# Turning the first token tile in front of the mixer by transfers and VectorE instead of TensorE

## The chip, the cores and the metric

The kernel runs on one core of a Trainium2 chip. A core has TensorE (PE in the profile; PEld is its weight load), VectorE (DVE), ScalarE (ACT), GpSimd (POOL), and queues that issue transfers (SP's above all). The engines run beside each other; each takes its own instructions strictly in the order in which they were written, and waits on semaphores for the others. PE writes to PSUM, from where ACT and DVE fetch. The metric is the device time of one execution in microseconds, the median over runs.

## The reference

Two layers over 256 tokens with 1024 features, all in float32. What surrounds the change, in each layer:

```python
h = layer_norm(ALPHA * h + 0.5 * swiglu(h, ffn1_gate[l], ffn1_up[l], ffn1_down[l]), ln_g[l, 0], ln_b[l, 0])
z = h @ w_in[l]
cb, cc, ch, rq, rf, ri, rg, pu = jnp.split(z, split_at, axis=-1)
...
f = lb + (1.0 - lb) * jax.nn.sigmoid(f_logit.astype(f32))
k = 1.0 - f
...
h = layer_norm(ALPHA * h + mix, ln_g[l, 1], ln_b[l, 1])
h = layer_norm(ALPHA * h + cross_attn(h, mem, ...), ln_g[l, 2], ln_b[l, 2])
h = layer_norm(ALPHA * h + 0.5 * swiglu(h, ffn2_gate[l], ...), ln_g[l, 3], ln_b[l, 3])
```

The mixer is what lies between z and mix: a short gated convolution, a gated recurrence with forget gate f and input k = 1 - f, and a pooling over windows.

## The kernel before

**Number format.** Each float32 operand of a product is split into a rounded high part and a low part that is the rest (`split`, L74 to L77: ACT casts, DVE subtracts). A product is the sum of high by high, high by low and low by high. Weights come from memory into one of six buffers `raw` of 128x1024 (`load`, L79), are split into `whi` and `wlo`, and the buffer is free once the DVE subtraction has read it. So the order on DVE also sets when the next load may be issued.

**Layout.** Tokens lie in two tiles of 128 (h[0], h[1], tokens on the partitions). For products over the features a tile must be turned, so that features lie on the partitions: xT, with high part xTh and low part xTl, 8 blocks of 128 features by 256 tokens. `transposed_half` (L196) turns four blocks of 128x128 on PE into a bank of PSUM and splits them from there; `transposed` (L204) does both halves. The second tile is turned with its tokens reversed (unit `jdn`). Banks of PSUM with the tag `acc` are four.

**Around the change.** `ffn` computes the first feed-forward block, whose last part is `finish` (L328). `finish` ends the down projection tile by tile: `tile_done(0)` adds, normalizes and writes h[0]; then `tile_done(1)` the same for h[1]. Amid the products for tile 1 stands `turn_first` (L343), which turns tile 0 on PE: 8 transposes. In layer 0 this goes through `transposed`; in layer 1 (`prompt`), through `later_split` (L335), where the rounding is done at once and the low parts (`low_part`, L349) are put into gaps of the normalization. `finish` returns a function that turns tile 1 later.

Then `keys` (L933) computes half of the attention's keys from the memory tokens, four groups of 16 or more products into `acc` banks, each fetched by `add` (L150): ACT copies one half to `sums`, DVE adds the other. Before the fourth group tile 1 is turned. Then `mixer` (L957) begins: `columns(1280, 512, ...)` loads w_in for f, splits it in four parts that are held behind the normalization (two of them behind the first turned half of tile 1), and multiplies with xT. PE's first product that needs xT stands there. `ev_f` (L985) then makes f (sigmoid on ACT, a multiply-add on DVE) and k = 1 - f on DVE (L993). `columns(768, ...)` and further loads of w_in follow in the same way.

The order on each engine is what a scheduler made of the program when it was built; `issue_after` only holds instructions behind a given one. Inside the mixer's recurrence PE's order is written by hand (L1054).

Elsewhere the kernel turns tiles by transfers already: four transfers deal the columns of a tile to the four groups of 32 partitions, and one DVE instruction transposes all blocks of 32x32 (`turn`, L520 to L531, for the feed-forward activations; L1231 and L1292 in the mixer).

Of the kernel before, what the change touches and what calls it, by code (L numbers as in the profile page):

```python
# [8 lines left out]
F32 = mybir.dt.float32  # L9
# [8 lines left out]
P = 128  # L18
# [42 lines left out]
def model(ctx: ExitStack, tc: tile.TileContext, t: dict, out: bass.AP):  # L61
# [133 lines left out]

    def transposed_half(src, i, j, dh, dl, unit=idn, keep=None):  # L196
        pt = acc((P, 4, P))
        for k in range(4):
            turns.append(nc.tensor.transpose(pt[:, k, :], src[:, (4 * j + k) * P : (4 * j + k + 1) * P], unit))  # L199
# [4 lines left out]
    def transposed(src, i, dh, dl, unit=idn, keep=None):  # L204
        for j in range(2):
            transposed_half(src, i, j, dh, dl, unit, keep)
            if not j:
                halfway.append(lows[-1])
# [118 lines left out]

    def finish(mm, y, scale, gb, units, last=False, junk=None, ahead=None, prompt=False):  # L328

# [19 lines left out]
        def low_part(w):  # L349
            lows.append(nc.vector.tensor_tensor(w[1], w[2], w[0].bitcast(F32), op=ALU.subtract))  # L350
# [3 lines left out]
        def tile_done(i):  # L354
# [10 lines left out]
            for c in pieces:  # L365
# [45 lines left out]
            for c in pieces:  # L411
# [3 lines left out]
                if last:  # L415
                    e = nc.scalar if c.start == 512 else nc.sync
                    e.dma_start(out[0, tok(i), c], h[i][:, c])

        if ahead is None:
            tile_done(0)  # L420
            tile_done(1)
        else:
            split(*ahead.todo[0])
            if prompt:
                nc.scalar.copy(ahead.todo[1][0], ahead.todo[1][2])
                held.append(ahead.todo[1])
            with tc.issue_after(lows[-1].ins):
                tile_done(0)
            with tc.issue_after(normed[-1].ins):
                if prompt:  # L430
                    split(*ahead.todo[2])
                    split(*ahead.todo[3])
                tile_done(1)
                if not prompt:
                    for x in ahead.todo[1:]:
                        split(*x)
            if prompt:
                with tc.issue_after(normed[-1].ins):
                    low_part(held.pop())
        return lambda keep=None: transposed(h[1], 1, xTh, xTl, units[1], keep)  # L440

# [34 lines left out]
    def ffn(l, name, n, pend=None, last=False, early=None, started=None, following=None):  # L476
        gate, up, down = (t[f"{name}_{x}"][l] for x in ("gate", "up", "down"))
        with tc.tile_pool(name="ffn", bufs=2, reuse_waits="tile") as fp:
# [445 lines left out]

            ahead = following() if following else None
            return ahead, finish(tail, ys, 0.5, gb, (idn, jdn) if name == "ffn1" else (pdn, pdn), last, None if last else squares, ahead, ahead is not None and name == "ffn1")


# [28 lines left out]
    def mixer(l, fill):  # L957
        w_in = t["w_in"][l]
        with tc.tile_pool(name="mix", bufs=1, reuse_waits="tile") as mp:

            def columns(c0, ncol, take, behind=lambda p: None, after=()):
                with ExitStack() as queued:
                    for x in after:
                        queued.enter_context(tc.issue_after(x.ins))
                    w = load(w_in, 0, NK, c0, ncol, hold=bool(after))
                    for n, x in enumerate(w.todo):
# [18 lines left out]
            def ev_f(p):  # L985
                c = slice(2 * p, 2 * p + 2)
                nc.scalar.activation(f[:, :, c, :], f[:, :, c, :], AF.Sigmoid)
                for hh in (2 * p, 2 * p + 1):
# [3 lines left out]
                    )  # L992
                nc.vector.tensor_scalar(  # L993
                    k[:, :, 2 * p : 2 * p + 2, :], f[:, :, 2 * p : 2 * p + 2, :], -1.0, 1.0,
                    op0=ALU.mult, op1=ALU.add,
                )
# [7 lines left out]
            def values_by_halves():  # L1004
                w = load(w_in, 0, NK, 1792, 512)
                for i in range(NT):
# [183 lines left out]
            products_of_others(1)  # L1190
            w_gate = load(w_in, 0, NK, 2304, 512)

# [106 lines left out]

            return project_back([slab(a) for a in (0, 6, 2, 4)], 3, gb, 1.0, idn)  # L1300

# [159 lines left out]
```

## Time and profile before

| | |
|---|---|
| median of 3 runs | 1064.27 us (1064.23 to 1064.66) |
| profiled execution: span from first to last instruction | 1061.1 us |
| TensorE busy in the span | 1051.2 us |
| ScalarE busy in the span | 662.0 us |
| bytes moved by transfers | 251.06 MB, mean 237 GB/s |
| layer 0: end of the first feed-forward block to the mixer | about 165 to 200 us |
| layer 1: the same | about 688 to 724 us |

The profiled execution has no time of its own beside its span; the timed runs lie 3.2 us above it. In the rows of the order of time the first number is the start in the span, the second the duration, then engine, line, operation, what is written<-what is read, and a count where equal instructions follow each other; in brackets stands the idle time before it and who ended it. In the rows of groups, the numbers behind the bar are the busy time of the group in us and the mean of one in ns.

### The profile page before, as it was taken

To read this page: it belongs to the slowest core of one execution; us is meant where nothing else is said; L and a number is where in the kernel's file an instruction comes from. 1 tells how busy PE (TensorE), PEld (TensorE's weight loads), DVE (VectorE), ACT (ScalarE), POOL (GpSimd) and SP (SyncE) were. 2 spreads that over 40 slices of the span, in tenths; PEclk is the share of its full clock that TensorE was granted. 3 is DMA by queue.
4 is the path that set the end of the run, shared out by engine and by line. 5 is a ranking of instruction groups with operands and counts; after the bars stand their busy time and mean duration, and the time that the engine had idled before them with its cause. 6 is when DMAs were issued, how large, how long until landed. Compare 5 with 4: busy or idle time off the path is not lost.

```text
span 1061.1 us, 16496 instructions
## 1 busy us (share of the span) xinstructions
PE 1051.2 (99%) x6014; PEld 934.8 (88%) x6014; DVE 933.2 (88%) x1246; ACT 662.0 (62%) x909; POOL 94.7 (9%) x128
## 2 busy tenths in 40 slices
PE   9999999999999999999999999999999999999996
PEld 7888888889899888889888888998998998888896
DVE  6998898989988789887898987999899787898787
ACT  6675775676557566655665656666774655675661
POOL 8002001000000001010001001010000000000001
PEclk9999999999999999999999999999999999999999
DMA  9999984854675589988789978866636675799971
GB/s 364 296 320 280 260 272 146 268 166 155 210 271 179 171 281 231 363 192 217 239 305 254 338 224 208 271 233 222 206 122 215 241 243 162 242 303 294 241 194 68
DMA packets 142306, 251.06 MB, mean 237 GB/s; under 512 B 11249, under 2 KB 51985, under 8 KB 142225
## 3 DMA queue, kind: packets, MB, share of 16 engines
q1 hardware_dynamic: 130656, 228.89, 65.0%
q0 software_dynamic: 10992, 19.94, 10.9%
q10 hardware_dynamic: 576, 1.18, 0.3%
q8 instruction: 47, 0.77, 0.3%
q14 instruction: 35, 0.28, 0.1%
HBM read 234.50 MB, written 1.05 MB: 222 GB/s over the span
## 4 chain that ended last, share of the span: by engine, by line
PE 92%; DVE 3%; DMA 2%; issue 2%; ACT 1%; POOL 0%; DVEq 0%; ACTq 0%; POOLq 0%
PE acc L132 61%; PE dn L132 27%; DVE wlo L76 2%; PE acc L199 1%; DMA raw<-in_ffn_gate_dram 1%; DMA raw<-in_ffn_down_dram 1%; ACT whi L75 0%; PE dn L1139 0%; DVE raw L702 0%; PE dn L1213 0%; DMA lng<-in_ln_g_dram 0%; DMA h<-in_x_dram 0%; DVE al L76 0%; PE acc L581 0%; DVE square L531 0%
## 5 line engine op out<-in xcount | busy, mean ns | idle before, releaser
L75 ACT CAST whi<-raw 128x1024 fp32r<-128x1024 f32 (+1 forms) x452 | 456.1, 1042 | 201.2 <-PE dn L132 58.0
L76 DVE TENSOR_TENSOR wlo<-raw,whi 128x1024 fp32r<-128x1024 f32 (+1 forms) x452 | 534.5, 1211 | 53.1 <-ACT whi L75 47.1
L132 PE MATMUL acc<-whi,xT 128*128 128x512 f32 (+1 forms) x1064 | 313.9, 372 | 0.0
L132 PEld LDWEIGHTS acc<-whi,xT 128*128 128x128 f32 x1064 | 199.0, 189 | 26.9 <-DVE xT L76 0.3
L132 PE MATMUL acc<-wlo,xT 128*128 128x512 f32 (+1 forms) x532 | 197.9, 372 | 0.0
L132 PE MATMUL dn<-whi,ah 128*128 128x512 f32 x346 | 131.5, 380 | 0.0
L132 PE MATMUL dn<-wlo,ah 128*128 128x512 f32 x346 | 131.3, 379 | 0.0
L132 PE MATMUL dn<-whi,al 128*128 128x512 f32 x346 | 131.1, 379 | 0.0
L132 PE MATMUL acc<-xT,whi 128*128 128x512 f32 x480 | 117.6, 381 | 0.0
L132 PEld LDWEIGHTS acc<-wlo,xT 128*128 128x128 f32 x532 | 100.6, 189 | 13.4
L132 PEld LDWEIGHTS acc<-xT,whi 128*128 128x128 f32 x480 | 86.8, 190 | 9.8
L132 PE MATMUL dn<-whi,xT 128*128 128x512 f32 x288 | 87.7, 380 | 0.0
L132 PEld LDWEIGHTS dn<-wlo,ah 128*128 128x128 f32 x346 | 65.4, 189 | 9.6 <-DVE wlo L76 0.6
L132 PEld LDWEIGHTS dn<-whi,al 128*128 128x128 f32 x346 | 65.4, 189 | 9.2
L132 PEld LDWEIGHTS dn<-whi,ah 128*128 128x128 f32 x346 | 65.4, 189 | 9.0
L132 PEld LDWEIGHTS acc<-xT,wlo 128*128 128x128 f32 x480 | 62.9, 191 | 3.2
L132 PE MATMUL acc<-xT,wlo 128*128 128x256 f32 x480 | 63.2, 275 | 0.0
L132 PE MATMUL acc<-wlo,kTh 128*128 128x512 f32 (+1 forms) x176 | 61.7, 351 | 0.0
L132 PE MATMUL acc<-whi,kTl 128*128 128x512 f32 (+1 forms) x176 | 61.7, 351 | 0.0
L132 PE MATMUL acc<-whi,kTh 128*128 128x512 f32 (+1 forms) x176 | 61.7, 351 | 0.0
L132 PEld LDWEIGHTS dn<-whi,xT 128*128 128x128 f32 x288 | 54.4, 189 | 7.6
L132 PE MATMUL dn<-wlo,xT 128*128 128x512 f32 x144 | 54.6, 379 | 0.0
(252 smaller groups left out, 1296.8 us busy)
## 6 DMA issues: line engine op xcount, KB each, us to landing
raw<-in_ffn_up_dram SPq DMA_DIRECT2D x88, 512.0 KB, 5.7
raw<-in_ffn_down_dram SPq DMA_DIRECT2D x88, 512.0 KB, 5.6
raw<-in_ffn_gate_dram SPq DMA_DIRECT2D x84, 512.0 KB, 5.6
raw<-in_w_in_dram SPq DMA_DIRECT2D x48, 512.0 KB, 4.8
dealt<-sg SPq DMA_DIRECT2D x80, 128.0 KB, 4.5
raw<-in_ffn_up_dram POOLq DMA_DIRECT2D x19, 512.0 KB, 6.3
raw<-in_ffn_gate_dram POOLq DMA_DIRECT2D x16, 512.0 KB, 9.4
raw<-in_ca_k_dram SPq DMA_DIRECT2D x16, 512.0 KB, 5.2
```

What stands on the lines that cost most here:

```text
L75: rounded = nc.scalar.copy(hi, src)
L76: lows.append(nc.vector.tensor_tensor(lo, src, hi.bitcast(F32), op=ALU.subtract))
L132: turns.append(nc.tensor.matmul(o, w, x, start=start, stop=stop, skip_group_check=more))
L199: turns.append(nc.tensor.transpose(pt[:, k, :], src[:, (4 * j + k) * P : (4 * j + k + 1) * P], unit))
```

## The change

In front of the mixer, in both layers:

- Tile 0 is no longer turned on PE. When h[0] is normalized, ACT copies it in two halves of 512 columns into a spare tile, with the features regrouped (every eighth column lies beside the next); four transfers on SP deal it to the four groups of 32 partitions in a second spare tile; after tile 1 is normalized, one DVE instruction transposes the blocks of 32x32 into a third; ACT rounds this into xTh and DVE takes the low part, both reading it with the tokens regrouped (a step of 32 floats).
- So block k of xT now holds the features k, k + 8, k + 16 and so on. Tile 1 is still turned on PE, but reads every eighth column of h[1]; w_in is loaded in the same order of features (`across`, eight rows of the matrix next to each other in a partition).
- In layer 1 the low part of the fourth key weight tile takes the place in the gap of the normalization that a low part of xT had.
- k = 1 - f is made by ACT, not DVE.

```diff
-    def transposed_half(src, i, j, dh, dl, unit=idn, keep=None):
+    def transposed_half(src, i, j, dh, dl, unit=idn, keep=None, grouped=False):
         pt = acc((P, 4, P))
-        for k in range(4):
-            turns.append(nc.tensor.transpose(pt[:, k, :], src[:, (4 * j + k) * P : (4 * j + k + 1) * P], unit))
+        for k in range(4 * j, 4 * j + 4):
+            of_k = src[:, k::NK] if grouped else src[:, k * P : (k + 1) * P]
+            turns.append(nc.tensor.transpose(pt[:, k - 4 * j, :], of_k, unit))
...
-                        None if last or not i or not n else turn_first,
+                        None if last or squares_of or not i or not n else turn_first,
...
+        def turn_by_squares():
+            x, y, o = squares_of()
+            for n in range(2):
+                c = slice(n * 512, n * 512 + 512)
+                nc.scalar.copy(
+                    y[:, c].rearrange("p (g k j) -> p g k j", g=2, j=32),
+                    h[0][:, c].rearrange("p (g j k) -> p g k j", g=2, j=32),
+                )
+            x = x.rearrange("p (b c) -> p b c", b=4)
+            for g in range(4):
+                nc.sync.dma_start(x[g * 32 : g * 32 + 32], y[:, g * 256 : (g + 1) * 256])
+            o = o.rearrange("p (k t) -> p k t", t=P)
+
+            def rest():
+                nc.vector.transpose(
+                    o.rearrange("p k (b r) -> p b k r", b=4), x.rearrange("p b (k j) -> p b k j", j=32)
+                )
+                split(
+                    *(y[:, :, tok(0)].rearrange("p k (r b) -> p k r b", b=4) for y in (xTh, xTl)),
+                    o.rearrange("p k (b r) -> p k r b", b=4),
+                )
+
+            return rest
+
         if ahead is None:
             tile_done(0)
+            rest = turn_by_squares() if squares_of else None
             tile_done(1)
+            if rest:
+                with tc.issue_after(normed[-1].ins):
+                    rest()
...
+                if squares_of:
+                    rest = turn_by_squares()
                 if prompt:
                     split(*ahead.todo[2])
-                    split(*ahead.todo[3])
+                    if squares_of:
+                        nc.scalar.copy(ahead.todo[3][0], ahead.todo[3][2])
+                        held.append(ahead.todo[3])
+                    else:
+                        split(*ahead.todo[3])
...
                 with tc.issue_after(normed[-1].ins):
-                    low_part(held.pop())
+                    if squares_of:
+                        rest()
+                    else:
+                        low_part(held.pop())
...
-                    w = load(w_in, 0, NK, c0, ncol, hold=bool(after))
+                    w = load(w_in, 0, NK, c0, ncol, hold=bool(after), across=True)
...
-                nc.vector.tensor_scalar(
-                    k[:, :, 2 * p : 2 * p + 2, :], f[:, :, 2 * p : 2 * p + 2, :], -1.0, 1.0,
-                    op0=ALU.mult, op1=ALU.add,
+                nc.scalar.activation(
+                    k[:, :, 2 * p : 2 * p + 2, :], f[:, :, 2 * p : 2 * p + 2, :], AF.Copy, scale=-1.0, bias=1.0
                 )
```

The other loads of w_in (for the values and the gate) get `across=True` too, and `squares_of` hands out three spare tiles of the feed-forward block's pool, named squares.

How it moves the instructions on the engines: first ACT in layer 0, from the squares of tile 0's normalization (the activation into kTh) on; h_72 is tile 0, h_73 tile 1. Before:

```order
L392 ACTIVATE kTh,mv<-h_72,mv 128x1024
L75 CAST whi<-raw 128x1024 x2
L75 CAST xT<-acc 128x4x128 x2
L75 CAST whi<-raw 128x1024 x3
L392 ACTIVATE kTh,mv<-h_73,mv 128x1024
L75 CAST whi<-raw 128x1024
L152 COPY sums<-acc 128x256 x2
L75 CAST kTh<-sums 128x512
L75 CAST xT<-acc 128x4x128
```

and the same place now:

```order
L393 ACTIVATE kTh,mv<-h_72,mv 128x1024
L424 COPY squares<-h_72 128x512
L75 CAST whi<-raw 128x1024
L424 COPY squares<-h_72 128x512
L75 CAST whi<-raw 128x1024 x4
L393 ACTIVATE kTh,mv<-h_73,mv 128x1024
L152 COPY sums<-acc 128x256
L75 CAST whi<-raw 128x1024
L152 COPY sums<-acc 128x256
L75 CAST xT<-squares 128x8x128
L75 CAST kTh<-sums 128x512
L75 CAST xT<-acc 128x4x128 x2
```

The two casts of tile 0 from PSUM are gone; two copies stand ahead of tile 1's squares, and one cast of the whole tile ahead of kTh and of tile 1's casts.

DVE in layer 0, from the last step of tile 1's normalization to the second key group's low part. Before:

```order
L412 SCALAR_TENSOR_TENSOR h_73<-h_73,rs,lnb 128x512 x2
L153 TENSOR_TENSOR sums<-acc,sums 128x256
L76 TENSOR_TENSOR wlo<-raw,whi 128x1024
L153 TENSOR_TENSOR sums<-acc,sums 128x256
L76 TENSOR_TENSOR wlo<-raw,whi 128x1024
L76 TENSOR_TENSOR kTl<-sums,kTh 128x512
L76 TENSOR_TENSOR xT<-acc,xT 128x4x128
L153 TENSOR_TENSOR sums<-acc,sums 128x256
L76 TENSOR_TENSOR xT<-acc,xT 128x4x128
L76 TENSOR_TENSOR wlo<-raw,whi 128x1024 x2
```

and now:

```order
L413 SCALAR_TENSOR_TENSOR h_73<-h_73,rs,lnb 128x512 x2
L434 STREAM_TRANSPOSE squares<-squares 128x4x8x32
L153 TENSOR_TENSOR sums<-acc,sums 128x256 x2
L76 TENSOR_TENSOR wlo<-raw,whi 128x1024
L76 TENSOR_TENSOR xT<-squares,xT 128x8x128
L76 TENSOR_TENSOR kTl<-sums,kTh 128x512
L76 TENSOR_TENSOR xT<-acc,xT 128x4x128 x2
L153 TENSOR_TENSOR sums<-acc,sums 128x256 x2
L76 TENSOR_TENSOR wlo<-raw,whi 128x1024 x2
L76 TENSOR_TENSOR kTl<-sums,kTh 128x512
L76 TENSOR_TENSOR wlo<-raw,whi 128x1024 x3
```

The transposing and the low part of tile 0 stand ahead of tile 1's low parts, and three of the four wlo of the mixer's first load have moved behind these.

DVE in layer 1, from the same step to tile 1's low parts. Before:

```order
L412 SCALAR_TENSOR_TENSOR h_73<-h_73,rs,lnb 128x512 x2
L350 TENSOR_TENSOR xT<-acc,xT 128x4x128
L153 TENSOR_TENSOR sums<-acc,sums 128x256
L76 TENSOR_TENSOR wlo<-raw,whi 128x1024
L153 TENSOR_TENSOR sums<-acc,sums 128x256
L76 TENSOR_TENSOR wlo<-raw,whi 128x1024
L76 TENSOR_TENSOR kTl<-sums,kTh 128x512
L76 TENSOR_TENSOR xT<-acc,xT 128x4x128 x2
```

and now:

```order
L413 SCALAR_TENSOR_TENSOR h_73<-h_73,rs,lnb 128x512 x2
L434 STREAM_TRANSPOSE squares<-squares 128x4x8x32
L153 TENSOR_TENSOR sums<-acc,sums 128x256
L76 TENSOR_TENSOR wlo<-raw,whi 128x1024
L76 TENSOR_TENSOR xT<-squares,xT 128x8x128
L153 TENSOR_TENSOR sums<-acc,sums 128x256
L76 TENSOR_TENSOR wlo<-raw,whi 128x1024
L76 TENSOR_TENSOR kTl<-sums,kTh 128x512
L76 TENSOR_TENSOR xT<-acc,xT 128x4x128 x2
```

The second add into sums, which frees a bank of PSUM, now stands behind the low part of the whole tile.

More of the change, by code (lines that the diff above doesn't have):

```diff
@@ L925, in ffn @@
             ahead = following() if following else None
-            return ahead, finish(tail, ys, 0.5, gb, (idn, jdn) if name == "ffn1" else (pdn, pdn), last, None if last else squares, ahead, ahead is not None and name == "ffn1")
+            return ahead, finish(tail, ys, 0.5, gb, (idn, jdn) if name == "ffn1" else (pdn, pdn), last, None if last else squares, ahead, ahead is not None and name == "ffn1", (lambda: [fp.tile([P, DM], F32, tag=f"spare{n}", name="squares", bufs=1) for n in range(3)]) if name == "ffn1" else None)
     def key_weights(l, c, hold=False):
```

16 lines of the change are left out of this document (9 added, 7 removed).

## The prediction

> **What bounds the kernel now.** I read first the head of the page, then who waits for whom on TensorE, then the instructions in order of time on each engine where the mixer begins.
>
> ```profile
> span 1061.1 us, 16496 instructions
> ...
> PE 1051.2 (99%) x6014; PEld 934.8 (88%) x6014; DVE 933.2 (88%) x1246; ACT 662.0 (62%) x909; POOL 94.7 (9%) x128
> ...
> PE dn L562 <- DVE kTh L557: 1.5, 1, 1.5
> PE acc L581 <- DMA h<-in_x_dram: 0.4, 1, 0.4
> ```
>
> The reader is to see that TensorE (PE) is busy 99% and waits for others only at the very start, 1.9 us in all. So work taken off PE shortens the run by what it took there, and any new wait of PE lengthens it one for one. VectorE (DVE), at 88%, has little room where its work is moved. The span is 1061.1 us and the median of the timed runs 1064.27; the 3.2 us between lie outside the span, and I add my sum to the median.
>
> **What is removed: eight transposes in each layer.** PE in order of time, layer 0, then the same place in layer 1:
>
> ```profile
> 170.96 1.04 PE L199 MATMUL acc<-idn,h 128*128 128x128 f32 x8
> 171.75 0.46 PE L132 MATMUL dn<-whi,ah 128*128 128x512 f32 x1
> 172.05 0.38 PE L132 MATMUL dn<-wlo,ah 128*128 128x512 f32 x1
> ...
> 185.78 1.67 PE L132 MATMUL acc<-xT,whi 128*128 128x512 f32 x7
> ...
> 693.94 1.04 PE L338 MATMUL acc<-idn,h 128*128 128x128 f32 x8
> ...
> 695.03 0.38 PE L132 MATMUL dn<-wlo,ah 128*128 128x512 f32 x1
> ...
> 705.27 1.04 PE L199 MATMUL acc<-jdn,h 128*128 128x128 f32 x8
> 706.06 1.76 PE L132 MATMUL acc<-mT,whi 128*128 128x512 f32 x7
> ```
>
> Products of 512 columns start (1.67 - 0.38)/6 = 0.22 us apart (seven of them at 185.78, one at 172.05). From 170.96 to 172.05 PE did the transposes and one product: 172.05 - 170.96 - 0.22 = **0.87 us** a layer, 1.75 in both (layer 1: 695.03 - 693.94 - 0.22 = 0.87). That is all the change can gain. The first product that needs xT starts at 185.78; without the transposes PE would be there at 184.91.
>
> **What is added: instructions that read with a step.** ScalarE (ACT) copies h with a step of 8 floats (2 x 512 columns); DVE transposes 128x1024 read contiguously; ACT rounds it and DVE takes the low part, both reading with a step of 32 floats. The rows next to these:
>
> ```profile
> L76 DVE TENSOR_TENSOR wlo<-raw,whi 128x1024 fp32r<-128x1024 f32 x36 | 43.1, 1218 | 1.6 <-ACT whi L75 1.2 <-DMA raw<-in_ca_k_dram 0.2
> L75 ACT CAST whi<-raw 128x1024 fp32r<-128x1024 f32 x38 | 38.6, 1052 | 5.1 <-PE dn L132 3.8 <-DMA raw<-in_w_in_dram 1.2
> L229 DVE STREAM_TRANSPOSE turned<-early 128x512 f32<-128x512 f32 x2 | 2.1, 1091 | 0.0
> L75 ACT CAST ah<-sg 128x256 fp32r<-128x256 f32 x2 | 1.6, 872 | 0.0
> L76 DVE TENSOR_TENSOR al<-sg,ah 128x256 fp32r<-128x256 f32 x2 | 1.6, 838 | 0.0
> L531 DVE STREAM_TRANSPOSE square<-dealt 128x512 f32<-128x512 f32 x2 | 1.3, 687 | 0.0
> L75 ACT CAST kTh<-sums 128x512 fp32r<-128x512 f32 x2 | 1.2, 617 | 1.9 <-DVE sums L153 1.9
> ```
>
> Contiguous, ACT takes 617 ns for 512 columns and 1052 for 1024: 0.85 ns a column and 0.18 us fixed; DVE by its 687 and 1218 takes 1.04 ns a column and 0.15 us. The split of ah reads s with a step of 4 floats (L804 to L808) and takes 872 and 838 ns for 256 columns: (872 - 180)/256 = (838 - 150)/256 = **2.7 ns a column** on both engines. L229 reads with a step of 8 floats: (1091 - 150)/512 = 1.84 ns. So:
> - copy of 512: from 0.62 (contiguous) to 1.56 us (2.7 ns). I take 1.14, by L229, which has the same step.
> - rounding of 128x1024: from 1.05 to 2.94; low part: from 1.22 to 2.90 us. I take 2.94 and 2.90, by the split of ah, which is the same pair of instructions with such a read.
> - transposing 128x1024: 0.15 + 1.04 x 1.024 = 1.22 us, as L531 reads and writes in the same way.
>
> **Layer 0: when xT is whole.** ACT, then DVE, in order of time before the change; starts in a queue lie 0.06 to 0.1 us closer than the durations say.
>
> ```profile
> 170.51 1.99 ACT L75 CAST whi<-raw 128x1024 fp32r<-128x1024 f32 x2 [2.31 <-PE dn L132]
> 172.41 1.07 ACT L75 CAST xT<-acc 128x512 fp32r<-128x512 f32 x2
> 173.37 2.96 ACT L75 CAST whi<-raw 128x1024 fp32r<-128x1024 f32 x3
> 176.21 1.16 ACT L392 ACTIVATE kTh<-h,mv 128x1024 fp32r<-128x1024 f32 x1
> ...
> 178.89 1.41 DVE L412 SCALAR_TENSOR_TENSOR h<-h,rs,lnb 128x512 f32<-128x512 f32 x2
> 180.22 0.41 DVE L153 TENSOR_TENSOR sums<-acc,sums 128x256 f32<-128x256 f32 x1
> 180.55 1.21 DVE L76 TENSOR_TENSOR wlo<-raw,whi 128x1024 fp32r<-128x1024 f32 x1
> ...
> 184.75 0.69 DVE L76 TENSOR_TENSOR xT<-acc,xT 128x512 fp32r<-128x512 f32 x1
> 185.36 2.35 DVE L76 TENSOR_TENSOR wlo<-raw,whi 128x1024 fp32r<-128x1024 f32 x2
> ```
>
> 1. ACT's queue now has copy, whi, copy, whi x4 ahead of the squares of tile 1: from 170.40, 1.06 + 0.95 + 1.06 + 3.80, so the squares start at 177.27, not 176.21. Tile 1's normalization on DVE hangs on them and ends 1.06 later; the transposing starts at 180.22 + 1.06 = 181.28 and ends at 182.4.
> 2. ACT rounds from 182.5 to 185.45; behind it queue kTh and both casts of tile 1. Meanwhile DVE does two sums and one wlo (2.0 us, hidden), then waits. Low part 185.5 to 188.3, kTl 0.60, the low part of tile 1's first half 0.60: 189.6.
> 3. PE's first product with xT starts at **189.6, not 185.78: +3.8**. The gain of 0.87 is in that, since PE only waits longer.
> 4. Before, the low parts of the four weight tiles were done by 187.7. Now one is done when PE starts; the next ends at 191.9 (0.6 + 0.67 + 1.13 later). PE's new order takes other products between them; followed row by row, waits of 0.2, 0.05 and 0.2 are left: +0.5. Layer 0: **+4.3 us**.
>
> **Layer 1.**
>
> ```profile
> 702.64 0.69 DVE L350 TENSOR_TENSOR xT<-acc,xT 128x512 fp32r<-128x512 f32 x1
> ...
> 704.71 0.42 DVE L153 TENSOR_TENSOR sums<-acc,sums 128x256 f32<-128x256 f32 x1
> ...
> raw<-in_w_in_dram SPq DMA_DIRECT2D x48, 512.0 KB, 4.8
> dealt<-sg SPq DMA_DIRECT2D x80, 128.0 KB, 4.5
> ```
>
> Here the normalization comes 0.87 earlier (702.64 - 0.87 = 701.8). Copies end at 694.5 and 696.5, SP issues the four transfers until 697.2, and by dealt<-sg (same size) the last lands 4.5 later, at 701.7: just in time. Transposing to 703.0, rounding 703.07 to 706.0, low part to 708.9. Behind it on DVE stands the second sums, which ends at 709.3, not 705.1. That add frees a bank of PSUM that PE's fourth group of key products needs: PE waits until **709.3, not 706.06: +3.2**, and nothing is late afterwards. Both layers: 4.3 + 3.2 = **+7.5 us**.
>
> **Edits that I cost at nothing.** k = 1 - f goes from DVE to ACT:
>
> ```profile
> 196.29 0.41 DVE L993 TENSOR_SCALAR k<-f 128x512 f32<-128x512 f32 x1
> ...
> 163.89 0.37 SPq L103 DMA_DIRECT2D raw<-in_w_in_dram  x1
> 172.85 1.50 SPq L103 DMA_DIRECT2D raw<-in_w_in_dram  x2
> ...
> L987 ACT ACTIVATE f<-f 128x512 f32<-128x512 f32 x2 | 1.3, 630 | 1.5 <-DVE f L153 1.4
> ```
>
> DVE gains 0.33 us twice a layer and ACT pays 0.63; PE waits for neither there. Without that cover it is worth -0.7 to +1.3 us a layer. On SP the transfers stand behind the four w_in loads of f, the last issued at 163.89. The copies end at 171.5 and 173.5, so SP is through with the four at 174.9, and the next load, issued at 172.85 before, waits for that; PE doesn't wait for its landing. Loads of w_in by contiguous rows of a partition move the same bytes in as many issues; their landing of 4.8 us could move by some tenths, which reaches PE through the weights of layer 0: between -0.5 and +1 us. POOL's memset of AT comes later and is needed 40 us later.
>
> The eight transposes of tile 1 now load their weights with a step of 8 floats. The rows show only contiguous ones:
>
> ```profile
> L199 PEld LDWEIGHTS acc<-jdn,h x16: 138/140/142, 182.1 to 705.9; 128*128 128x128 f32 x16
> ```
>
> They start 0.1 us apart (0.79 us for eight). By the 2.7 ns a column above, a load would take 0.35, and eight 2.0 us more a layer; by the moving side nothing, as products that pick columns 256 floats apart run at the 0.22 us spacing. In the forecast both ends cost 0: PE has 3 to 4 us of waiting right behind them. If that cover is gone they cost up to 1.7 us. The Trainium skill, "Advanced Engine Details and Errata", section "SBUF Cachelines", says that reads which go to a different 16-byte line each time are penalized, whichever engine reads; by that rule the loads pay the 2.0 us, without it 0. No row here shows it for weights.
>
> **The rivals.**
> 1. *Not slower: the steps cost nothing here.* Copies 0.62, rounding 1.05, low part 1.22. Layer 0: ACT isn't later, the transposing ends at 181.4, and two sums, wlo, low part, kTl and tile 1's first low part (4.1 us) end at 185.5, 0.3 before 185.78; the wlo of step 4 are then late by 1.2 to 1.4: +1.0. Layer 1: the second sums ends at 705.9: -0.2. Together +0.8: 1065.0. Between this and the next rival it decides at about 1.25 ns a column, where the sum passes 2.1 us. Against it: 872 and 838 ns for 256 columns.
> 2. *The milder step*, 1.84 ns everywhere: rounding and low part 2.06 each, +2.7 and +1.5: 1068.5.
> 3. *DVE hides it all.* If xT and the banks were ready when PE comes (184.9 and 705.2; my chains end 4.7 and 4.1 us later), only the transposes would be left: 1064.27 - 1.75 = 1062.5. The chain is one queue on DVE with nothing to drop, which speaks against it.
> 4. *PE's clock falls back* in the waits. At the start PE takes twice as long:
>
> ```profile
> 4.41 1.09 PE L581 MATMUL acc<-pdn,h 128*128 128x128 f32 x4 [0.38 <-DMA h<-in_x_dram]
> 6.68 1.04 PE L581 MATMUL acc<-pdn,h 128*128 128x128 f32 x8
> core 0: 1061.1 us, clock 0.998
> ```
>
> Four transposes took what eight take later, and a mean of 0.998 is 2.1 us lost. A second such stretch in each layer costs up to 2.1 each: 1064.27 + 7.5 + 4.2 = 1076.0. The Trainium skill, "TensorE: Matmul & The Clock Gate", section "HAM oscillation — how this bites in real kernels", puts the point at an idle gap of about 3.4 us; by that rule my waits of 3.8 and 3.2 us straddle it.
>
> **How the numbers follow.** Forecast +7.5 (2.7 ns): 0.45, 1071.8. Milder step: 0.25. Clock or a transfer that lands later than 4.5: 0.10. No cost of steps: 0.15. All hidden: 0.05. A difference under 0.2% (2.1 us) can't be told from no change. Slower: 0.45 + 0.25 + 0.10 = 0.80; within: 0.17, from the last two; faster 0.03, if the gain is larger than the rows show. The range leaves out the last case and the far end of the clock: 1065.0 to 1075.5.
>
> **What would show it.** The casts and low parts of xT from the transposed tile at 2.9 us, copies at 1.1; PE waiting some 3.8 us for the low part of xT in layer 0 and some 3.2 us for sums in layer 1, and nowhere else. Casts near 1.1 us would prove the steps wrong; a PE wait on wlo or on a transfer, the order of my steps.

## The result, and the profile after

| | before | with the change |
|---|---|---|
| median of 6 runs each | 1063.91 us (1062.95 to 1064.66) | 1067.1 us (1066.95 to 1068.52) |
| ratio | | 1.0033 (1.0022 to 1.0045) |
| span of the profiled execution | 1061.1 us | 1066.8 us |

The change makes the kernel 3.2 us slower by the medians; the ratio gives 3.5 us, between 2.3 and 4.8. The forecast was 7.5 us. The head of the page after, and all of TensorE's waits (engine, what it wanted to write, line; who it waited for; us in total, times, longest):

```profile
span 1066.8 us, 16483 instructions
...
PE 1052.6 (99%) x5998; PEld 934.3 (88%) x5998; DVE 936.6 (88%) x1242; ACT 670.6 (63%) x915; POOL 95.0 (9%) x128
```

```profile
PE acc L132 <- DVE sums L153: 1.9, 1, 1.9
PE acc L132 <- DVE xT L76: 1.7, 1, 1.7
PE dn L600 <- DVE kTh L595: 1.5, 1, 1.5
PE acc L619 <- DMA h<-in_x_dram: 1.0, 2, 0.6
PE acc L200 <- DVE sums L153: 0.6, 1, 0.6
```

Before, the list held only kTh (1.5) and h (0.4). Three waits are new, 4.2 us in all. In layer 0 the second half of tile 1's turning (L200) waits for a bank that an add of `sums` frees, and the first product with xT waits for xT's low part; in layer 1 the fourth group of key products waits for a bank. Here they stand in order of time; ACT, DVE and PE of layer 0:

```profile
170.86 1.15 ACT L424 COPY squares<-h 128x512 f32<-128x512 f32 x1 [2.21 <-DVE h L413]
...
177.69 1.16 ACT L393 ACTIVATE kTh<-h,mv 128x1024 fp32r<-128x1024 f32 x1
...
182.96 2.12 ACT L75 CAST xT<-squares 128x1024 fp32r<-128x1024 f32 x1 [2.55 <-DVE squares L434]
...
181.69 1.24 DVE L434 STREAM_TRANSPOSE squares<-squares 128x1024 f32<-128x1024 f32 x1
182.85 0.72 DVE L153 TENSOR_TENSOR sums<-acc,sums 128x256 f32<-128x256 f32 x2
...
185.11 2.01 DVE L76 TENSOR_TENSOR xT<-squares,xT 128x1024 fp32r<-128x1024 f32 x1 [0.41 <-ACT xT L75]
187.04 0.67 DVE L76 TENSOR_TENSOR kTl<-sums,kTh 128x512 fp32r<-128x512 f32 x1
187.63 1.28 DVE L76 TENSOR_TENSOR xT<-acc,xT 128x512 fp32r<-128x512 f32 x2
...
183.29 0.71 PE L200 MATMUL acc<-jdn,h 128*128 128x128 f32 x4 [0.65 <-DVE sums L153]
...
188.37 1.78 PE L132 MATMUL acc<-xT,whi 128*128 128x512 f32 x7 [1.75 <-DVE xT L76]
```

And of layer 1:

```profile
708.48 1.95 DVE L76 TENSOR_TENSOR xT<-squares,xT 128x1024 fp32r<-128x1024 f32 x1 [0.79 <-ACT xT L75]
710.35 0.41 DVE L153 TENSOR_TENSOR sums<-acc,sums 128x256 f32<-128x256 f32 x1
...
707.90 1.04 PE L200 MATMUL acc<-jdn,h 128*128 128x128 f32 x8
710.82 2.34 PE L132 MATMUL acc<-mT,whi 128*128 128x512 f32 x7 [1.87 <-DVE sums L153]
```

The chain is the one that the prediction walked: copies, squares of tile 1, transposing, rounding, low part, and behind it kTl and tile 1's low part in layer 0, the second add of `sums` in layer 1. But rounding takes 2.12 and 2.16 us and the low part 2.01 and 1.95, not 2.94 and 2.90. The copies take 1.15 us each, as forecast. The four transfers land 2.8 to 3.2 us after their issue and are never waited for.

Not all of the loss stands in the list of waits: 4.2 less the 1.75 us of transposes would be 2.5. In layer 0 the low parts of w_in are late too (step 4 of the prediction). The first line is the kernel before, the second the change, the third a group of the page after (weight loads of the products of xT with these low parts), which waits 0.9 us for `wlo`; before, no such wait stood there:

```profile
193.42 1.89 PE L132 MATMUL acc<-xT,whi 128*128 128x512 f32 x8
```

```profile
196.59 1.89 PE L132 MATMUL acc<-xT,whi 128*128 128x512 f32 x8
```

```profile
L132 PEld LDWEIGHTS acc<-xT,wlo 128*128 128x128 f32 x480 | 63.4, 191 | 4.2 <-DVE wlo L76 0.9
```

Ahead of these lines TensorE did the same 47 products with xT: from 185.78 to 193.42 before, 7.64 us, and from 188.37 to 196.59 now, 8.22 us. These 0.58 us and the three waits, less the transposes, make 3.0 to 3.1 us.

The two spans differ by more than the medians do. The changed kernel's profiled execution is its slowest of six. Its time is 1.7 us above its span, and by the same 1.7 us the profiled execution before took 1062.8 us, below all six of its runs. So differences between traces are up to 2.5 us larger here than those between medians; where it matters, below, I compare medians.

### The profile page after: what moved, and what is told of

Its sections match the earlier page's. It is cut to its first block, busy times and chain, and to the rows that moved or that the text cites. A ratio compares the mean times of both kernels' runs of the same rounds, so it can differ in the third digit from the quotient of the medians.

```text
span 1066.8 us, 16483 instructions
## 1 busy us (share of the span) xinstructions
PE 1052.6 (99%) x5998; PEld 934.3 (88%) x5998; DVE 936.6 (88%) x1242; ACT 670.6 (63%) x915; POOL 95.0 (9%) x128
## 3 DMA queue, kind: packets, MB, share of 16 engines
HBM read 234.50 MB, written 1.05 MB: 221 GB/s over the span
## 4 chain that ended last, share of the span: by engine, by line
PE 95%; ACT 2%; DVE 2%; issue 1%; DMA 1%; ACTq 0%; DVEq 0%
PE acc L132 63%; PE dn L132 30%; PE acc L200 1%; ACT whi L75 1%; DMA h<-in_x_dram 1%; PE dn L1176 0%; DVE xT L76 0%; ACT xT L75 0%; PE dn L1250 0%; DVE h L413 0%; ACT kTh L393 0%; DVE h L408 0%; PE dn L1238 0%; PE dn L1249 0%; PE acc L1318 0%
```

## The experiments

Differences are against runs of the kernel before on the same chip. My first theory: the steps were overpriced, the other edits cost nothing, and TensorE's three waits, with small gaps in layer 0, are the whole loss.

**1. The change once more.**

> The change as it is, to see how far one execution differs from another. By my theory (PE is held up three times, 0.65 and 1.75 us in layer 0 and 1.87 us in layer 1, and about 0.9 us go into small gaps in layer 0, against 1.75 us of transposes saved) this gives +3.4 us against the kernel before in every execution, and the 1.5 us that TensorE lost at half clock behind the wait of layer 1 are an accident of the one profiled execution: a second profile shows the same three waits and a clock of 1.00 between 711 and 716 us. The rival (the wait itself lets the clock fall) expects the same half clock in the second profile, and +5 us.

1066.51 us against 1063.57: ratio 1.0031 (1.0020 to 1.0042). The second profile shows the same waits; below, TensorE in layer 1, and the windows behind the wait, first of this run and then of the first profile (from to, us, busy of each engine, granted clock, DMA share, GB/s):

```profile
710.57 1.78 PE L132 MATMUL acc<-mT,whi 128*128 128x512 f32 x7 [1.89 <-DVE sums L153]
```

```profile
709.70:714.70 5.00, 4.13 (x23) 3.76 (x24) 5.00 (x8) 4.15 (x7) 0.00 (x0) 1.00 0.77 268
```

```profile
711.00:716.00 5.00, 5.00 (x20) 4.46 (x21) 4.43 (x7) 3.74 (x7) 0.00 (x0) 0.66 0.58 191
```

The clock is 1.00 here and was 0.66 there, behind the same wait. So the fallback is an accident of an execution and not the loss of the median; the 3.4 us expected are inside the interval of 2.1 to 4.5.

**2. All but the turning.** Both tiles on TensorE, tile 0 too with every eighth column:

```diff
+        grouped, squares_of = squares_of is not None, None
...
+                of_k = h[i][:, 4 * j + k :: NK] if grouped else h[i][:, (4 * j + k) * P : (4 * j + k + 1) * P]
...
-                transposed(h[0], 0, xTh, xTl, units[0])
+                transposed(h[0], 0, xTh, xTl, units[0], grouped=grouped)
```

> All of the change but the turning: both tiles are turned on TensorE (tile 0 too with every eighth column as weights), w_in is loaded by contiguous rows, ScalarE makes k. My theory: these edits cost nothing, so within 0.5 us of the kernel before, and the 16 transposes of tile 0 with stepped weights stand at the same spacing as before (1.04 us for eight, 0.87 us of time with the product behind them). Rival: the loads of w_in, k on ScalarE or the stepped weights carry part of the loss; then +1 to +2 us, or 1.7 us a layer if a stepped weight load takes 0.35 us.

1063.95 us, ratio 1.0003 (0.9994 to 1.0011): no difference. None of the three waits is there. The stepped weight loads (rows by line, ns min/median/max) are longer than the contiguous ones (138/140/142 for the same loads before), but the transposes are not, and eight of them stand at the old spacing (1.04 us in the row of 707.90 above):

```profile
L200 PEld LDWEIGHTS acc<-jdn,h x16: 185/191/193, 182.6 to 707.1; 128*128 128x128 f32 x16
L200 PE MATMUL acc<-jdn,h x16: 272/274/276, 182.8 to 707.2; 128*128 128x128 f32 x16
```

So w_in's loads, k on ScalarE and stepped weights cost nothing that can be measured (-0.6 to +1.2 us).

**3. k back on VectorE.**

```diff
-                nc.scalar.activation(
-                    k[:, :, 2 * p : 2 * p + 2, :], f[:, :, 2 * p : 2 * p + 2, :], AF.Copy, scale=-1.0, bias=1.0
+                nc.vector.tensor_scalar(
+                    k[:, :, 2 * p : 2 * p + 2, :], f[:, :, 2 * p : 2 * p + 2, :], -1.0, 1.0,
+                    op0=ALU.mult, op1=ALU.add,
```

> The change with k = 1 - f back on VectorE. My theory: the time of the change within 0.5 us, with the same waits of TensorE. Rival (ScalarE late with k or with what stands behind it): 0.7 to 1.3 us a layer less; or, if VectorE is the bound there, up to 0.7 us a layer more.

1066.84 us, ratio 1.0034 (1.0022 to 1.0047): the time of the change, with the same waits (1.8, 1.7, 0.6). The move of k is free.

**4. The split reads in order.**

```diff
-                split(
-                    *(y[:, :, tok(0)].rearrange("p k (r b) -> p k r b", b=4) for y in (xTh, xTl)),
-                    o.rearrange("p k (b r) -> p k r b", b=4),
-                )
+                split(xTh[:, :, tok(0)], xTl[:, :, tok(0)], o)
```

> The change, but the split of the transposed tile reads it in order (no step of 32 floats), so the tokens of tile 0 stand permuted in xT. My theory: rounding 1.05 us instead of 2.12, low part 1.2 instead of 2.0, so what hangs on them comes 1.8 us earlier: the wait for xT in layer 0 (1.75 us) and the wait for sums in layer 1 (1.87 us) fall to under 0.3 us each, the wait of 0.65 us for sums in layer 0 stays, and the time is 3.0 to 3.6 us below the change, so within 0.6 us of the kernel before. Rival (the steps are not what holds TensorE up; the transfers or the order on VectorE do): less than 1 us below the change.

This kernel leaves out the reordering of tile 0's tokens, so only its time is of use. 1064.62 us, ratio 1.0009 (1.0000 to 1.0018): 1.9 us below the change by the medians. The rows of the tile `squares`, and TensorE's waits:

```profile
L75 ACT CAST xT<-squares x2: 1047/1057/1067, 182.7 to 705.0; 128x1024 fp32r<-128x1024 f32 x2
L76 DVE TENSOR_TENSOR xT<-squares,xT x2: 1214/1214/1214, 184.3 to 706.3; 128x1024 fp32r<-128x1024 f32 x2
```

```profile
PE acc L200 <- DVE sums L153: 0.6, 1, 0.6
...
PE acc L132 <- DVE xT L76: 0.5, 1, 0.5
PE acc L132 <- DVE sums L153: 0.3, 1, 0.3
```

Both long waits fall, by 1.2 and 1.6 us, and the third stays, as my theory has it. The amount is a miss: 3.0 to 3.6 were expected. By the spans of the two profiles (1065.0 and 1062.2 us) it is 2.8. In layer 0 part of what xT gains goes to the late low parts of w_in: the 47 products with xT take 8.48 us here instead of 8.22.

**5. The low part behind the add of sums.** Only layer 1's order on VectorE (the lines that set it):

```diff
+            if prompt and squares_of:
+                with tc.issue_after(adds[-2].ins):
+                    low_part(held.pop())
```

> The change, but in layer 1 the low part of the turned tile stands on VectorE behind the second add of the key sums, not in front of it. My theory: TensorE's fourth group of key products waits 1.87 us for the bank that this add frees; the add now runs at about 707.7 us, before the rounding is done at 708.4, so the low part isn't later, the wait falls to under 0.2 us and no other wait comes: 1.9 us below the change. Rival (the chain itself is late, and the wait only moves to the first product that needs xT): less than 0.5 us below the change, with a wait for xT in layer 1.

1067.21 us, ratio 1.0036 (1.0022 to 1.0050): nothing gained, the rival is right. TensorE's waits:

```profile
PE acc L132 <- DVE xT L76: 2.0, 2, 1.7
...
PE acc L132 <- DVE wlo L76: 1.0, 1, 1.0
PE acc L200 <- DVE sums L153: 0.6, 1, 0.6
...
PE acc L132 <- DVE sums L153: 0.3, 1, 0.3
```

The wait for the bank is down to 0.3, but in its place stand 0.3 for xT (the 2.0 are two, 1.7 in layer 0) and 1.0 for a weight's low part, and the 47 products with xT take 9.15 us in layer 1 instead of 7.64. VectorE goes through one list there; whatever is taken forward pushes the rest back, and TensorE wants all of it.

**6. No copies.** h[0] is dealt, the transposing reads every eighth column:

```diff
-            x, y, o = squares_of()
-            for n in range(2):
-                c = slice(n * 512, n * 512 + 512)
-                nc.scalar.copy(
...
+            x, _, o = squares_of()
+            y = h[0]
...
-                    o.rearrange("p k (b r) -> p b k r", b=4), x.rearrange("p b (k j) -> p b k j", j=32)
+                    o.rearrange("p k (b r) -> p b k r", b=4), x.rearrange("p b (j k) -> p b k j", j=32)
```

> The change without ScalarE's two copies: h[0] itself is dealt, and VectorE's transposing reads every eighth column (2.0 us instead of 1.24, by 1.84 ns a column). My theory: in layer 0 the copies hold back the rounding of weights, VectorE waits for that in front of tile 1's sums, and so the normalization is late; without them it ends some 2.4 us earlier, the transposing some 1.7 us earlier, and the waits of 0.65 and 1.75 us fall to under 0.3 us together. In layer 1 the copies hold back nothing, and the wait for sums grows by the 0.8 us of the slower transposing, to 2.6. In all 1.3 to 1.9 us below the change. Rival (the copies cost nothing, the long chain on VectorE does): layer 0 stays as it is or gets 0.8 us longer, and the time is 0.8 to 1.6 us above the change.

1068.16 us, ratio 1.0048 (1.0035 to 1.0061), so slower than the change by the medians: a miss. DVE, and the waits:

```profile
179.33 2.05 DVE L429 STREAM_TRANSPOSE squares<-squares 128x1024 f32<-128x1024 f32 x1
```

```profile
PE acc L132 <- DVE sums L153: 2.6, 1, 2.6
PE acc L132 <- DVE xT L76: 1.7, 1, 1.7
```

The transposing takes 2.05, layer 1's wait grows to 2.6, and in layer 0 the transposing starts 2.4 us earlier (2.0 with the 0.36 us taken off by which the change's execution ran late) and the wait of 0.65 is gone, all as expected. But the wait for xT is still 1.7. TensorE, not held up ahead of it, also comes earlier, and its first product with xT stands 1.1 us earlier than in the change. About half of that goes at once: the 47 products with xT now take 8.76 us, not 8.22. Layer 1 loses 0.7 us more. So these traces show no gain; why the median is 1.7 us above the change's they don't show.

**7. The transposing amid the normalization**, with the order of 5:

```diff
+            with tc.issue_after(centred.ins):
+                amid()
```

> As the run with the low part behind the sums, and in both layers the transposing stands on VectorE amid tile 1's normalization (layer 0: between its last two instructions; layer 1: where the schedule puts it behind the first pass). My theory: in layer 0 the rounding on ScalarE now runs beside VectorE's last normalization and adds, xT is ready about 1.4 us earlier, and its wait of 1.75 falls to 0.4; the turning of tile 1 waits for the normalization and the bank, 0.9 to 1.2 us instead of 0.65. Layer 1 as in that run. In all 2.5 to 3.2 us below the change, so within 0.6 us of the kernel before. Rival (the delayed normalization costs as much as the early rounding brings): like the run with the low part behind the sums.

1067.73 us, ratio 1.0042 (1.0030 to 1.0055): a miss. The wait for xT falls to 0.9 in layer 0, but 0.8 us for h[1] and 1.7 us for low parts of weights come up. As in 5, an order moves the wait and does not remove it.

**8. Steps by themselves.** Ten pairs at the end of the kernel before; the eight with one step n:

```diff
+            split(
+                *(y.rearrange("p (k j) -> p k j", k=n) for y in (rounded, low)),
+                stepped.rearrange("p (j k) -> p k j", k=n),
+            )
```

> The kernel before with ten pairs of rounding and low part of 128x1024 at its end, which read with steps of 1, 2, 4, 8, 16, 32, 64 and 128 floats, and in the two patterns of the kernel (runs of 32 with a step of 4, as in the split of s; runs of 4 with a step of 32, as in the split of the turned tile). It adds some 30 us of its own. My theory: the price hangs on the step, and 4 floats is the dear one: 1.05 us at 1, 1.6 at 2, 2.95 at 4, and 2.0 to 2.1 from 8 up, on both engines; the two patterns like their steps. Rival (the 872 ns of the split of s come from its small size, 0.4 us fixed): 2.1 us at a step of 4 too. A third (a step costs more, the longer it is): rising from 8 to 128.

ScalarE's rows of steps 1, 2, 4 and 32, then the runs of 32 with a step of 4; VectorE's of 1 and 4:

```profile
1060.09 1.04 ACT L75 CAST rounded<-stepped 128x1024 fp32r<-128x1024 f32 x1 [17.50 <-DVE stepped L1437]
1061.04 1.12 ACT L75 CAST rounded<-stepped 128x1024 fp32r<-128x1024 f32 x1
1062.07 2.03 ACT L75 CAST rounded<-stepped 128x1024 fp32r<-128x1024 f32 x1
...
1067.85 1.96 ACT L75 CAST rounded<-stepped 128x1024 fp32r<-128x1024 f32 x1
...
1073.50 2.06 ACT L75 CAST runs<-stepped 128x1024 fp32r<-128x1024 f32 x1
...
1061.17 1.23 DVE L76 TENSOR_TENSOR low<-stepped,rounded 128x1024 fp32r<-128x1024 f32 x1 [1.19 <-ACT rounded L75]
...
1064.13 2.03 DVE L76 TENSOR_TENSOR low<-stepped,rounded 128x1024 fp32r<-128x1024 f32 x1 [0.60 <-ACT rounded L75]
```

My theory misses at 2 (1.6 forecast, 1.12 measured) and at 4 (2.95 and 2.03), and the third one, that longer steps cost more, falls. The rival's 2.1 us at a step of 4 comes in; its reason, a large fixed time, is tried in 12. A step of 2 floats costs next to nothing, and from 4 floats on every step costs the same: 1.96 to 2.07 us on ScalarE against 1.04, some 1.8 ns a column. The step of 4, from which the forecast had 2.7 ns, is no dearer than the step of 32.

**9 to 11. The keys' low parts on GpSimd**, alone, with the order of 5, and in an attempt at a faster version:

```diff
-            split(kTh[:, d, :], kTl[:, d, :], o)
+            nc.scalar.copy(kTh[:, d, :], o)
+            (nc.vector if c else nc.gpsimd).tensor_tensor(
+                kTl[:, d, :], o, kTh[:, d, :].bitcast(F32), op=ALU.subtract
+            )
```

> The change, but the low parts of the keys (kTl, two of 0.67 us in each layer, needed only by the attention much later) are made by GpSimd, which is 91% idle, not by VectorE. Theory of the backlog: behind the normalization VectorE works through one list without a gap but the wait for the rounding, and TensorE is held up by whatever stands too late in it; work that leaves the list comes back whole: 0.6 to 1.3 us a layer, 1.2 to 2.6 in all, in layer 1 too, though kTl stands there behind the add that TensorE waits for. Theory of the single chain (only what stands ahead of the awaited instruction counts): in layer 0 kTl stands ahead of tile 1's low part, so its wait falls from 1.75 to 1.1; in layer 1 the wait of 1.87 for sums stays as it is: 0.6 us in all. GpSimd's own time for 128x512 isn't in any row; up to 10 us would be in time.

> Both: the keys' low parts on GpSimd, and in layer 1 the low part of the turned tile behind the second add of sums. Theory of the backlog: layer 1 then waits 0.3 us for the bank, and the 0.27 and 0.97 us that came up for xT and wlo in the run with the add ahead fall by the 1.3 us taken off VectorE, to nothing; layer 0 as with the keys on GpSimd. In all 2.0 to 3.0 us below the change, 0 to 1 us above the kernel before. Rival (the waits move on again): less than 1 us below the change.

> An attempt at a version that beats both: no copies (h[0] itself is dealt, the transposing reads every eighth column), the transposing put ahead of the last pass of tile 1's normalization, the low part behind the second add of sums in layer 1, the keys' low parts on GpSimd. By the backlog: the transposing and part of the adds fill the 1.7 us in which VectorE waits for ScalarE's squares only if the transfers have landed (about 176.5 us in layer 0, 702.5 in layer 1); rounding then runs beside the normalization. TensorE's waits fall to under 1.0 us a layer in layer 0 and under 0.5 in layer 1, against 0.87 saved in each: within 0.7 us of the kernel before. Rival (wlo of the weights stands ahead of tile 1's low part in the new order and keeps TensorE waiting for xT): 1 to 2 us above the kernel before.

1070.11, 1071.6 and 1068.85 us, ratios 1.0070 (1.0056 to 1.0084), 1.0075 (1.0062 to 1.0087) and 1.0050 (1.0037 to 1.0062): all slower than the change by the medians, all misses. POOL, ACT and PE of the first, in layer 0:

```profile
185.34 2.52 POOL L980 TENSOR_TENSOR kTl<-sums,kTh 128x512 fp32r<-128x512 f32 x1 [5.46 <-ACT kTh L979]
...
187.89 0.37 ACT L152 COPY sums<-acc 128x256 f32<-128x256 f32 x1 [1.67 <-POOL kTl L980]
...
189.46 3.01 PE L132 MATMUL acc<-xT,whi 128*128 128x512 f32 x7 [3.16 <-DVE xT L76]
```

The kernel has one buffer for `sums`. GpSimd reads it for 2.52 us where VectorE took 0.67; ScalarE's next copy into it waits, then VectorE's add behind that copy, and tile 1's low part behind the add. The wait for xT grows to 3.16 us, and behind it the clock falls (x7 in 3.01 us instead of 1.67). I had counted VectorE's list and not what the moved instruction holds. So layer 0 says nothing for or against the backlog. In layer 1 ScalarE waits only 0.24 us for GpSimd, and TensorE's wait for `sums` stays at 1.82 us, as the theory of the single chain had it. A version with a second buffer wasn't run, and what made 10 and 11 slow wasn't taken apart.

**12. Steps by size.** Pairs at the end of the kernel before:

```diff
+                    *(y[:, 0:size].rearrange("p (k j) -> p k j", k=n) for y in (rounded, low)),
+                    stepped[:, 0:size].rearrange("p (j k) -> p k j", k=n),
```

> The kernel before with pairs of rounding and low part at its end for 256 and for 512 columns: in order, with a step of 4, with a step of 32, and in runs of 32 with a step of 4 as in the split of s; behind them two roundings of 256 with that pattern by ScalarE alone. From 128x1024 (2.03 us at a step of 4) and the copies of 128x512 (1.15): 0.27 us fixed and 1.72 ns a column, so 0.71 us at 256 in the theory that a price by the column holds and the 872 and 838 ns of the split of s are its own; rival: every stepped instruction has a larger fixed part, 0.45 us, and 256 columns take 0.87 here too. In order 0.37 to 0.42 us at 256 and 0.62 to 0.69 at 512.

The pattern of the split of s (runs of 32, step 4), for 256 and 512 columns, with min/median/max:

```profile
L75 ACT CAST runs<-stepped x2: 643/878/1113, 1060.5 to 1063.5; 128x256 fp32r<-128x256 f32 x1, 128x512 fp32r<-128x512 f32 x1
L76 DVE TENSOR_TENSOR runs_low<-stepped,runs x2: 621/853/1085, 1061.1 to 1064.7; 128x256 fp32r<-128x256 f32 x1, 128x512 fp32r<-128x512 f32 x1
```

643 and 1113 ns, with 2.06 us for 1024: about 0.18 us and 1.83 ns a column. Neither the form nor the size makes the 872 and 838 ns of the split of s: the price goes by the column, as the first theory says, a little below its 0.71 us for 256, and the rival's large fixed part falls.

**13. The place of that split.** More such pairs behind it, on s and on another tile:

```diff
+                    other = wp.tile([P, 1024], F32, tag="raw", name="other", bufs=6)
...
+                    for n, x in (("again", s), ("other", other.rearrange("p (j c) -> p j c", j=4)), ("again", s)):
```

> The kernel before; behind the split of s at about 160 us the same pair of instructions (256 columns, runs of 32 with a step of 4 floats) is done twice on s again, twice on another tile filled with ones, and twice on s once more, into weight buffers that nobody reads. At the end of the kernel, where transfers rest, this form took 643 to 657 ns on ScalarE and about 620 on VectorE. Theory of the surroundings (transfers busy 95% of this stretch slow a stepped read): 840 to 890 ns on both tiles. Theory of the tile (where s lies): 840 to 890 on s, 620 to 660 on the other. If both take 620 to 660, it was the first reading of fresh data. The time of the run says nothing, since weights come later by it.

```profile
L75 ACT CAST ah<-sg x2: 640/641/642, 151.2 to 151.8; 128x256 fp32r<-128x256 f32 x2
L76 DVE TENSOR_TENSOR al<-sg,ah x2: 604/606/608, 151.9 to 152.5; 128x256 fp32r<-128x256 f32 x2
```

```profile
151.10:152.60 1.50, 0.00 (x0) 0.00 (x0) 0.74 (x3) 1.37 (x3) 0.00 (x0) 0.72 0.00 0
```

The split of s itself now takes 641 and 606 ns. So it isn't the tile, and not fresh data. But the added instructions held up the weights, so TensorE (first busy time) and the transfers (DMA share, ahead of the last number) stood still in the window. In the kernel before the window of the same split reads:

```profile
157.80:159.50 1.70, 1.70 (x9) 1.51 (x8) 1.50 (x2) 1.70 (x4) 0.00 (x0) 1.00 0.65 170
```

There TensorE was busy without a gap and the transfers had a share of 0.65. The surroundings made the row dear; which of them, this run can't tell. A busy TensorE and busy transfers don't do it to every stepped read: beside both (transfers 0.76) a stepped copy of the change, at 696.65, took 1.15 us, where 512 stepped columns took 1.11 at the quiet end of the kernel (12).

**14. No step at all**: 4, and copies in order.

```diff
+                nc.scalar.copy(y[:, c], h[0][:, c])
```

> The change with no step at all: copies and split read in order, so features and tokens of tile 0 stand permuted in xT. By the prediction's first rival +0.8 us against the kernel before; by the run with the split alone in order (+1.05 us) less what two copies of 0.62 instead of 1.15 us let go on ScalarE: the weights' rounding in layer 0 comes 1.0 us earlier, so the wait of 0.65 us for sums falls to 0.1 and the wait of 0.5 for xT to 0.1: 0.3 to 0.9 us above the kernel before. Rival (the copies of ScalarE cost nothing): the time of the run with the split alone in order, within 0.3 us.

1063.04 us against 1063.19, ratio 0.9997 (0.9988 to 1.0006). TensorE's waits, without the 1.5 us at the start:

```profile
PE acc L132 <- DVE xT L76: 0.5, 1, 0.5
...
PE dn L132 <- DVE wlo L76: 0.4, 1, 0.4
PE acc L132 <- DVE sums L153: 0.3, 1, 0.3
```

As in 4, the tokens (and now the features) of tile 0 are left out of order. The bank's wait of 0.65 is gone, as expected of the copies; the wait of 0.5 for xT stays, and the time is below the 0.3 to 0.9 us that were forecast, though its interval reaches to +0.6. The rival's time, that of run 4, is outside the interval. With 4 (+1.05 us, here -0.15) the copies' step is worth 1.2 us and the split's 1.9, each with about 1.5 us either way, so that the copies' share alone isn't clear of noise: together 3.1, as much as the loss of the change.

No version that keeps tile 0 in order beat the kernel before. What the change could gain is 1.75 us of transposes, and even without a step no gain can be measured. The trace of 14 shows where it goes. Without the 0.11 us by which it ran late, the first product with xT in layer 0 stands 0.2 us earlier than before the change, but the 47 products from there on take 8.40 us instead of 7.64.

## Why the prediction was wrong

- **What bounds the kernel**: right. TensorE stays at 99%, and its new waits, with the late low parts of w_in in layer 0, are the loss.
- **Removed, 0.87 us a layer**: right. In run 14, where the steps are gone, TensorE's waits and the late low parts still eat it up.
- **Rounding 2.94 and low part 2.90: the step that failed.** They measured 2.12 to 2.16 and 1.95 to 2.01. The price of 2.7 ns a column was taken from one row of 256 columns, by subtracting the fixed time of contiguous instructions. Measured alone, the same form costs 1.8 ns, and the row was dear by its surroundings (12, 13); what in them did it stays open. The copies, priced by L229 at 1.84 ns, were right: 1.14 forecast (0.18 us and 512 times 1.84 ns make 1.12), 1.15 measured. The prediction so had the right price in its rows, and used it for the copies and the second rival only.
- **Layer 0**: with the measured durations, step 3 of the forecast gives 189.6 - 0.82 - 0.92 = 187.9 instead of 185.78. In the profile TensorE begins at 188.37, and this execution ran 0.45 us late from its start: 187.9. The order, the squares 1.06 later (1.04 measured) and tile 1's low part in the chain were right. So was step 4, the late low parts of w_in: 0.5 us forecast, 0.58 measured; only the list of signs had left its wait out. The wait of 0.65 for a bank I had not seen; it costs nothing of its own, since TensorE would only have waited longer for xT.
- **Layer 1**: the same correction makes 707.6 of 709.3. In the profile it is 710.82, and less the 3.24 us by which this execution stands later at the start of the stretch (699.78 against 697.41 - 0.87), 707.6. The wait for the bank stands where it was forecast, 1.87 us. "Nothing is late afterwards" held only since the wait was that long: run 5 shows that without it xT and a weight are late.
- **The sum** by the right price is 7.5 - 3.5 = 4.0 us. Measured are 3.2 by the medians, between 2.3 and 4.8.
- **Rivals**: the milder step (1068.5 us) came nearest. *The steps cost nothing* is wrong of this kernel, where the steps cost about 3 us. What it forecast for a kernel without that cost, +0.8 us, can be held against run 14: -0.15 (-1.3 to +0.6). Its mechanism shows there, xT in time in layer 0 (0.2 us early, 0.3 forecast) and the low parts of w_in late (0.76 us against 1.2 to 1.4), its price is too high. That VectorE hides it all fell. The clock fell back in one of two profiles, behind a wait of 1.87 us, and not as a rule.
- **The transfers** land in 2.8 to 3.2 us, not 4.5, and so are not "just in time" in layer 1; it changed nothing.
- **Edits costed at nothing**: k, w_in's loads and the stepped weights cost nothing that can be measured (2, 3), by experiment and not only by cover. The forecast's 3.2 us between span and median were wrong as "outside the span": 1.7 are outside, and the rest is the profiled execution being a quick one.

## What to carry to other kernels

Take the price of an access pattern from several rows of several sizes, and where only one small instruction has it, measure it alone: a term of 2.7 ns that was 1.8 here nearly doubled the forecast (7.5 us; 4.0 by the right price). Work taken from a full engine to a nearly full one comes back as waits, and reordering the nearly full one only moves them; what helps is less work on it and ahead of it (here: reads without a step, 3.1 us). Before an instruction goes to a slow idle engine, ask which buffer it holds meanwhile.

## What the runs showed of the hardware

- A float32 read with a step of 2 costs 1.12 us instead of 1.04 for 128x1024 on ScalarE, with any step from 4 to 128 floats 1.96 to 2.07; VectorE 1.22, 1.22 and 1.90 to 2.03. The Trainium skill, "Advanced Engine Details and Errata", section "SBUF Cachelines", has lines of 16 bytes, wants two hits on a line, and gives a penalty where each access goes to another line; that a step of 2 is cheap and a step of 4 dear agrees. That longer steps cost no more is shown by these rows alone. TensorE's weight loads with a step of 32 bytes took 191 instead of 140 ns (medians), and the transposes behind them did not slow.
- The same stepped instruction took 857 to 886 ns beside a busy TensorE and busy transfers, and 641 with both still. What does it is open: other stepped reads beside a busy TensorE and transfers were hardly dearer (1.15 us for a copy of 512 columns, against 1.11 at the quiet end).
- Behind a wait of 1.87 us TensorE's clock was 0.66 over 5 us in one execution; behind one of 1.89 us in another it was 1.00, as it was behind the 2.63 us of run 6. Behind the 3.16 us of run 9 it was 0.66. The Trainium skill, "TensorE: Matmul & The Clock Gate", section "HAM oscillation — how this bites in real kernels", puts the limit at idle gaps of some 3.4 us; in both of these falls the wait was shorter.
